# One small tile to the front, two padded: every SBUF tile of 1 KB or more starts at the same place modulo 256 bytes

## The chip, the cores and the metric

The kernel runs on one core of a Trainium2 chip. The metric is the device time of one execution in microseconds (us). The core has a matrix engine (TensorE, PE in the profile; its weight loads are listed apart, as PEld), a vector engine (VectorE, DVE), a scalar engine (ScalarE, ACT), GpSimd (POOL) and a queue engine (SyncE, SP). They work on SBUF, which has 128 partitions; a tile takes the same range of bytes in every partition, so a tile has one start address. Matmul results go to a separate memory, PSUM.

## What is computed

The reference is a one-layer encoder on a sequence of 1024 tokens with 1024 channels, all in float32. With depth 1 only the Hyena mixer is used, then a SwiGLU block, then a final norm:

```python
h = rmsnorm(x, norm_mix)
z = short_conv(h @ w_in + b_in, conv_w, conv_b)        # 1024 -> 3072, width 3
x0, x1, v = split(z, 3)
s = v * x1
g = hyena_filter(...)                                   # two-sided filter, L1-normalised
y = irfft(rfft(s, 2 * L) * rfft(g, 2 * L))[:L]          # long convolution
x = x + ((y + s * skip) * x0) @ w_out + b_out
x = x + (silu(u @ w_gate) * (u @ w_up)) @ w_down        # u = rmsnorm(x, norm_ffn), hidden 2816
return rmsnorm(x, norm_final)
```

## The kernel before

**Products.** Almost all of the work of TensorE is one kind of product. A float32 operand is split in a high part (a float32r copy, by ScalarE) and a low part (the difference, by VectorE or by an accumulating DMA on GpSimd's queue), and three products high·high, high·low and low·high are summed in PSUM. One such matmul takes a 128x128 block as stationary operand (the weight load) and streams a moving operand of 512 columns past it. The kernel has 4308 of these wide float32r matmuls, at six lines:

- lines 140, 356 and 683 (`gemm`, `piece`, `second_half`): z, the projection to 3072 channels, 1152 matmuls. The moving operand is the normed input, held in four tiles `uh0`, `uh1`, `ul0`, `ul1`; the stationary one is a block of `w_in` in a tile `whl`, which stands in the slot `whl0` or `whl1` (once in `cr`).
- line 895 (`out_mm`): po, the product with `w_out`, 384 matmuls. Here the `uh`/`ul` tiles are stationary and the `w_out` parts `wohl` are moving.
- line 1153 (`Unit.product`): the gate and up products. 22 units (`wg0` to `wg10`, `wu0` to `wu10`) of seven products `a` to `g`, of 12 matmuls each: 1848. The split weight is stationary and is put in turn in the five slots `fwd2`, `vz`, `s1`, `xz`, `sT` (`OPS`). The moving operand is `uh`/`ul`, or one of the sums T1 (slots `ab_g`, `gg0`), T2 (`cr`, `fwd01`), T3 (`whl1`, `hs`, `wt`).
- line 1397 (`mms`): bx, by and bz, the down products, 924 matmuls. The hidden values `hop` are stationary, `w_down` in `wop` is moving; both go through four pairs of slots in turn (`SETS`: `gg1`/`ab_d`, `hw`/`ss`, `inv`/`whl0`, and the pair `x0`,`ct_g` / `s0`,`ct_d`).

The other matmuls are narrower: transforms of 128 columns (lines 530, 531, 604, 643, 644), filter taps of 256 columns (513, 514) and transposes.

**Stages.** Up to about 430 us the kernel goes through eight channel blocks, one `period(b)` each: filter taps (ph), the filter's transform (pg), the turned signal (pst), its transform (pp), a butterfly on VectorE, the inverse transform (py) of the block before, and in between the z products of the next blocks, in stretches of 12, 6, 30 and 96 wide matmuls. Then the po products with the residual sum and the second norm (to about 557 us), the gate and up products (to about 955 us), and the down products with the final norm. The order on each engine is written out by hand (`manual_schedule`).

**Where tiles stand.** The pool `sb` gives each tag one slot (`bufs=2`: two), laid out in the order in which the tags are first asked for; a slot takes its size rounded up to 32 bytes. So one small tile in the row shifts all slots behind it. The start addresses that follow, modulo 256:

| slots | start modulo 256 before |
|---|---|
| `uh0`, `uh1`, `ul0`, `ul1`, `ident` | 128 |
| `fwd01`, `fwd2`, `ct_g`, `ct_d`, `ab_d`, `ab_g`, `x0`, `gg0`, `gg1`, `ss`, `cr`, `inv`, `wt`, `hs` | 96 |
| `junk`, `fw`, `dc`, `sT` | 128 |
| `s0`, `s1` | 192 |
| `xz`, `whl0`, `vz`, `whl1`, `fwh`, `fwl`, `hw` | 0 |

All offsets used inside these tiles by the wide matmuls are multiples of 512 bytes, so a matmul's two operands start modulo 256 where their slots start. In 784 of the 4308 wide matmuls the two starts are equal modulo 256 (432 of line 1153, 352 of line 1397), in the other 3524 they differ.

The small tiles that the change touches are `turn` (4 bytes, a factor for the filter's sine, used at line 709 and in `mlp_turns`), and the scratch of the norms, `rstd_of` (line 172 on, tags `rs1` and `rs2`) and `normed` (line 1038 on, tag `rs1`).

Of the kernel before, what the change touches and what calls it, by code (L numbers as in the profile page):

```python
# [102 lines left out]
def hyena_ffn_kernel(ctx: ExitStack, tc: tile.TileContext, a: dict, out: bass.AP):  # L103
# [18 lines left out]
    def small(name, *shape, tag=None, bufs=1, dt=F32):  # L122
        return sb.tile([P, *shape], dt, tag=tag or name, name=name, bufs=bufs)
# [38 lines left out]
    ones = small("ones", 1)  # L162
    V.memset(ones, 1.0)
    epst = small("epst", 1)
    V.memset(epst, EPS)
    warm = small("warm", 1)
    S.sqrt(warm, ones)

    def rstd_of(ss, n, nm):
        w = small(nm, 3 * n, tag=f"rs{n}", bufs=2)  # L170
        rt, r0, q = (w[:, i * n : (i + 1) * n] for i in range(3))
        S.activation(rt, ss, AF.Sqrt, bias=epst)
        V.reciprocal(r0, rt)
        V.scalar_tensor_tensor(q, ss, EPS, r0, ALU.add, ALU.mult)
        V.scalar_tensor_tensor(q, q, -0.5, r0, ALU.mult, ALU.mult)
        V.scalar_tensor_tensor(r0, q, 1.5, r0, ALU.add, ALU.mult)
        return r0
# [99 lines left out]
    rs = {}  # L277

    def rstd(j, n=1):
        r = rstd_of(sums[:, j : j + n], n, f"ra{j}")  # L280
        for q in range(n):
            rs[j + q] = r[:, q : q + 1]
# [41 lines left out]
            stop=True,  # L324
        )

    turn = small("turn", 1)

    def mlp_turns(li):
        ar = half(ark, li)  # L330
# [587 lines left out]
    b, f = NB - 1, F_[NB - 1]  # L918
# [117 lines left out]
        tops[nm] = (hi, lo)  # L1036

    def normed(j):
        w = small(f"rq{j}", 4, tag="rs1", bufs=2)
        sc, rt, r0, q = (w[:, i : i + 1] for i in range(4))  # L1040
        V.scalar_tensor_tensor(sc, sq2[j][:, 1:2], 1.0 / D, sq2[j][:, 0:1], ALU.mult, ALU.add)
        S.sqrt(rt, sc)
        V.reciprocal(r0, rt)
        V.scalar_tensor_tensor(q, sc, -0.5, r0, ALU.mult, ALU.mult)
        V.tensor_tensor(q, q, r0, ALU.mult)
        V.scalar_tensor_tensor(r0, q, 1.5, r0, ALU.add, ALU.mult)
        for h in range(2):
            d = x1[j][:, h * 512 : (h + 1) * 512]
            V.scalar_tensor_tensor(d, d, r0, gffn[:, h * 512 : (h + 1) * 512], ALU.mult, ALU.mult)
# [167 lines left out]
    with tc.manual_schedule(  # L1217
# [3 lines left out]
        for n, j in enumerate(seq):  # L1221
# [18 lines left out]
            if n < 7:  # L1240
                post_late()
                normed(j)
# [13 lines left out]
        ug.sums(V)  # L1256
        low_dma(pq[:, 0, 0], pq[:, 0, 1], ug.a12)
        normed(7)
        early_op(pq[:, 1], uu_.a12)
        ug.p1(pre[:, 0])  # L1260
# [263 lines left out]
```

## Time and profile before

| | |
|---|---|
| median of 3 runs (lowest, highest) | 1206.6 us (1204.96, 1207.47) |
| the profiled execution's own time | 1206.03 us |
| its span, first to last instruction | 1204.2 us |
| mean granted TensorE clock | 0.994 of full speed |
| PE busy | 1178.9 us, 98% of the span |
| DVE, ACT, POOL busy | 876.2, 516.1, 151.6 us |

The profile lists groups of instructions by source line and tile names (buffer numbers left out), with count, busy time and mean duration of one. Matmuls overlap in the pipeline and their ends are modelled, so the duration of one (near 390 ns for a wide one) is longer than the distance between the starts of two; the pace is read from start to start.

### The profile page before, as it was taken

To read this page: it belongs to the slowest core of one execution; us is meant where nothing else is said; L and a number is where in the kernel's file an instruction comes from. 1 tells how busy PE (TensorE), PEld (TensorE's weight loads), DVE (VectorE), ACT (ScalarE), POOL (GpSimd) and SP (SyncE) were. 2 spreads that over 40 slices of the span, in tenths; PEclk is the share of its full clock that TensorE was granted. 3 is DMA by queue.
4 is the path that set the end of the run, shared out by engine and by line. 5 is a ranking of instruction groups with operands and counts; after the bars stand their busy time and mean duration, and the time that the engine had idled before them with its cause. 6 is when DMAs were issued, how large, how long until landed. Compare 5 with 4: busy or idle time off the path is not lost.

```text
span 1204.2 us, 15168 instructions
## 1 busy us (share of the span) xinstructions
PE 1178.9 (98%) x5728; PEld 973.1 (81%) x5728; DVE 876.2 (73%) x1414; ACT 516.1 (43%) x818; POOL 151.6 (13%) x216
## 2 busy tenths in 40 slices
PE   8999999999999999998999999999999989999997
PEld 6788898888988887776888888888888868888885
DVE  6788989889898894588747666566656467955675
ACT  6564543545445472465233322332323233334444
POOL 0011211112011140043101110011001101111000
PEclk9999999999999999999999999999999999999999
DMA  7555667777575799443313332223323359832323
GB/s 218 158 114 130 144 162 161 166 152 164 125 154 108 199 244 262 132 114 70 131 44 123 100 128 88 88 97 122 105 71 108 111 180 350 311 117 92 96 79 140
DMA packets 100568, 170.32 MB, mean 141 GB/s; under 512 B 7052, under 2 KB 60684, under 8 KB 100367
## 3 DMA queue, kind: packets, MB, share of 16 engines
q0 software_dynamic: 24832, 78.39, 28.0%
q1 hardware_dynamic: 75661, 90.96, 22.8%
q8 instruction: 45, 0.74, 0.3%
q14 instruction: 28, 0.23, 0.1%
q10 hardware_dynamic: 2, 0.00, 0.0%
HBM read 101.96 MB, written 40.11 MB: 118 GB/s over the span
## 4 chain that ended last, share of the span: by engine, by line
PE 51%; DVE 3%; DMA 2%; ACT 1%; issue 1%; POOL 0%; SPq 0%; ACTq 0%; POOLq 0%
PE bx L1397 9%; PE by L1397 5%; PE bz L1397 3%; PE wg0dc L1153 1%; DMA hrp<-hd 1%; PE po L895 1%; PE wg1dc L1153 1%; PE wu8dc L1153 1%; PE wu5dc L1153 1%; PE wu3dc L1153 1%; PE wg6dc L1153 1%; PE wu7dc L1153 1%; PE wu2dc L1153 1%; PE wu9dc L1153 1%; PE wg5dc L1153 1%
## 5 line engine op out<-in xcount | busy, mean ns | idle before, releaser
L140 PE MATMUL z<-uh,whl 128*128 128x512 f32 x704 | 199.1, 398 | 0.2 <-DVE vz L386 0.2
L140 PEld LDWEIGHTS z<-uh,whl 128*128 128x128 f32 x704 | 130.4, 189 | 28.7 <-PE ph L514 0.4
L1397 PE MATMUL bx<-wop,hop 128*128 128x512 f32 x480 | 113.2, 394 | 1.4 <-ACT hop L129 1.1
L140 PE MATMUL z<-ul,whl 128*128 128x512 f32 x352 | 110.1, 394 | 0.0
L1397 PEld LDWEIGHTS bx<-wop,hop 128*128 128x128 f32 x480 | 89.9, 188 | 23.6 <-ACT hop L129 1.5
L130 DVE TENSOR_TENSOR hop<-hrp,hop 128x1024 fp32r<-128x1024 f32 (+1 forms) x40 | 45.1, 1129 | 52.1 <-ACT hop L129 52.0
L129 ACT CAST hop<-hrp 128x1024 fp32r<-128x1024 f32 (+1 forms) x40 | 38.9, 975 | 95.3 <-PE bx L1397 46.9
L895 PE MATMUL po<-wohl,uh 128*128 128x512 f32 x256 | 77.0, 403 | 2.0 <-DVE sig L659 1.8
L140 PEld LDWEIGHTS z<-ul,whl 128*128 128x128 f32 x352 | 66.3, 188 | 15.6
L1008 POOL DMA_DIRECT2D hd<-g x40 | 21.7, 545 | 332.8 <-DVE g L1313 193.7
L1397 PE MATMUL by<-wop,hop 128*128 128x512 f32 x264 | 61.5, 394 | 0.0
L895 PEld LDWEIGHTS po<-wohl,uh 128*128 128x128 f32 x256 | 48.1, 191 | 13.9 <-DVE sig L659 2.0
L1397 PEld LDWEIGHTS by<-wop,hop 128*128 128x128 f32 x264 | 49.6, 188 | 11.5
L190 ACT CAST whl<-wt 128x1024 fp32r<-128x1024 f32 x24 | 25.1, 1048 | 69.4 <-PE z L140 67.2
L129 ACT CAST wop<-wd 128x512 fp32r<-128x512 f32 x73 | 42.3, 617 | 18.7 <-PE by L1397 9.5
L150 POOL DMA_DIRECT2D whl<-wt x24 | 20.8, 872 | 229.2 <-ACT whl L149 218.8
L531 PE MATMUL pg<-hw,fwd 128*128 128x128 f32 x256 | 49.5, 275 | 0.0
L530 PE MATMUL pg<-hw,fwd 128*128 128x128 f32 x256 | 49.5, 275 | 0.0
L130 DVE TENSOR_TENSOR wop<-wd,wop 128x512 fp32r<-128x512 f32 x73 | 47.6, 685 | 2.0 <-ACT wop L129 2.0
L1008 POOL DMA_DIRECT2D hrp<-hd x42 | 22.4, 534 | 191.3 <-DVE hop L130 170.6
L895 PE MATMUL po<-wohl,ul 128*128 128x512 f32 x128 | 45.5, 400 | 0.0
L530 PEld LDWEIGHTS pg<-hw,fwd 128*128 128x128 f32 x256 | 39.5, 192 | 0.7
(1584 smaller groups left out, 2847.1 us busy)
## 6 DMA issues: line engine op xcount, KB each, us to landing
hrp<-hd POOLq DMA_DIRECT2D x35, 512.0 KB, 4.1
wt<-in_hy_w_in_dram SPq DMA_DIRECT2D x24, 512.0 KB, 4.9
whl<-wt POOLq DMA_DIRECT2D x24, 512.0 KB, 4.5
wgr<-in_ffn_w_gate_dram SPq DMA_DIRECT2D x22, 512.0 KB, 4.0
wur<-in_ffn_w_up_dram SPq DMA_DIRECT2D x22, 512.0 KB, 4.1
wd<-in_ffn_w_down_dram SPq DMA_DIRECT2D x44, 256.0 KB, 6.4
hd<-g POOLq DMA_DIRECT2D x40, 256.0 KB, 2.6
hd<-sx POOLq DMA_DIRECT2D x30, 256.0 KB, 2.7
```

The costliest lines, as they stand in the source:

```text
L129: S.copy(hi, src)
L130: (eng or V).tensor_tensor(lo, src, hi.bitcast(F32), ALU.subtract)
L140: T.matmul(pt[:, h * 512 : (h + 1) * 512], w[wi], u2[ui][h][:, k, :], start=first and ti == 0, stop=last and ti == len(TERMS) - 1,)
L150: G.dma_start(lo.bitcast(F32), src, accum_op=ALU.add)
L190: S.copy(whl[:, 0], w_raw[n])
L530: T.matmul(o, fwd[r][:, j, :], f.hw[:, j, 0, :], start=True, stop=False)
L531: T.matmul(o, fwd[2 * r][:, jj, :], f.hw[:, jj, 1, :], start=False, stop=True)
L895: T.matmul(o, u2[yi][th][:, k, m * P : (m + 1) * P], wos[h][k // 2][wi][:, k % 2, :], start=(k == 0 and ti == 0), stop=(k == NB - 1 and ti ...
L1008: G.dma_start(dst, src)
L1153: T.matmul(pt, t[:, wi, k, :], b(k)[ui], start=first and k == 0 and ti == 0, stop=k == 3 and ti == len(TERMS) - 1, skip_group_check=not first,
L1397: T.matmul(pt, ho[hi_][:, x, q * P : (q + 1) * P], wo_[wi][:, x, :], start=fresh and first and x == 0 and ti == 0, stop=last and x == n - ...
```

## The change

The tag `turn` is now asked for with the first small tiles, ahead of `fwd01`, instead of behind `hs`. That pushes `fwd01` to `hs` up by 32 bytes and leaves what comes behind where it was. The scratch tiles `rs1` and `rs2` (two buffers each) grow from at most 24 to 128 bytes, of which only the first few are used as before: `s0` and `s1` move up by 192 bytes, `xz` and all behind it by 384.

```diff
     epst = small("epst", 1)
+    turn = small("turn", 1)
     V.memset(epst, EPS)
...
     def rstd_of(ss, n, nm):
-        w = small(nm, 3 * n, tag=f"rs{n}", bufs=2)
+        w = small(nm, 32, tag=f"rs{n}", bufs=2)
...
-    turn = small("turn", 1)
...
     def normed(j):
-        w = small(f"rq{j}", 4, tag="rs1", bufs=2)
+        w = small(f"rq{j}", 32, tag="rs1", bufs=2)
```

Every slot of the table above then starts at 128 modulo 256. Modulo 512 they start at 128 too, but for `s0` and `s1`, which start at 384. Both operands of all 4308 wide matmuls start equal modulo 256; in 392 of them (those with `s0` or `s1`) they differ by 256 modulo 512. Each engine's list of instructions, with its shapes, waits and order, is the same as before; only addresses differ. The 1-column operands move too: `cp` from 224 to 0, the norms' scratch and the last small tiles by some bytes.

## The prediction

> **What bounds the kernel now.** First the page's head and busy shares:
>
> ```profile
> span 1204.2 us, 15168 instructions
> PE 1178.9 (98%) x5728; PEld 973.1 (81%) x5728; DVE 876.2 (73%) x1414; ACT 516.1 (43%) x818; POOL 151.6 (13%) x216
> PEclk9999999999999999999999999999999999999999
> ```
>
> TensorE works 98% of the span at the full granted clock. A change that moves only addresses shortens the kernel if it shortens matmuls, lengthens it if it lengthens them, and nothing else weighs as much. So the second view is the groups of matmuls by line:
>
> ```profile
> L140 PE MATMUL z<-uh,whl 128*128 128x512 f32 x704 | 199.1, 398 | 0.2 <-DVE vz L386 0.2
> L140 PE MATMUL z<-ul,whl 128*128 128x512 f32 x352 | 110.1, 394 | 0.0
> L530 PE MATMUL pg<-hw,fwd 128*128 128x128 f32 x256 | 49.5, 275 | 0.0
> L644 PE MATMUL py<-inv,vv 128*128 128x128 f32 x128 | 24.7, 275 | 0.0
> ```
>
> The z products, 1056 at this line, waited 0.2 us in all. The last two rows settle the narrow matmuls: pg pairs `hw` (0) with `fwd` (96), py pairs `inv` with `vv` (both 96), unequal against equal start, and both take 275 ns. Only the wide ones can be touched.
>
> The third view is the same group list for the gate and up stage, where each product is a row of its own and the five weight slots give every pairing of starts:
>
> ```profile
> L1153 PE MATMUL wg3ab<-uh,wg3b 128*128 128x512 f32 x8 | 2.7, 396 | 0.0
> L1153 PE MATMUL wu1ab<-uh,wu1b 128*128 128x512 f32 x8 | 2.7, 395 | 0.0
> L1153 PE MATMUL wg7ab<-uh,wg7a 128*128 128x512 f32 x8 | 2.7, 394 | 0.0
> L1153 PE MATMUL wu4ab<-T2h,wu4f 128*128 128x512 f32 x8 | 2.6, 390 | 0.0
> L1153 PE MATMUL wu3ab<-uh,wu3b 128*128 128x512 f32 x8 | 2.6, 390 | 0.0
> L1153 PE MATMUL wg2ab<-uh,wg2a 128*128 128x512 f32 x8 | 2.6, 390 | 0.0
> L1397 PE MATMUL bx<-wop12s,hop12x 128*128 128x512 f32 x8 | 3.2, 395 | 0.0
> L1397 PE MATMUL bx<-wop12ct_d,hop12x 128*128 128x512 f32 x8 | 3.1, 390 | 0.0
> ```
>
> Wg3b stood in `s1` (192), wu1b in `vz` (0), both against `uh` (128): 395 to 396 ns. Wg2a and wu3b stood in `sT` (128), equal to `uh`: 390. Wu4f in `fwd2` against T2 in `cr` and `fwd01`, 96 and 96: 390 too, so it is the equality and not the place. The last two rows are the cleanest: the same stationary blocks in `x0` (96) at the same time, with the moving part in `s0` (192) or in `ct_d` (96): 395 against 390. Wg7a, in `sT` like wg2a, shows 394; it is the exception that has to be explained. Single products by themselves, with minimum, median and maximum:
>
> ```profile
> L1153 PE MATMUL wg2ab<-uh,wg2a x8: 389/389/396, 613.2 to 615.7; 128*128 128x512 f32 x8
> L1153 PE MATMUL wg7ab<-uh,wg7a x8: 389/394/398, 808.2 to 811.2; 128*128 128x512 f32 x8
> L1153 PE MATMUL wu1ab<-uh,wu1b x8: 392/394/404, 615.9 to 618.5; 128*128 128x512 f32 x8
> ```
>
> Wg2a runs at a constant 389, with one exception; wu1b, unequal, wanders between 392 and 404 and never reaches 389. Wg7a reaches 389 but not at once: with equal starts the matmuls fall into a fast pace after some matmuls (I read none to ten of the twelve), and until then they wander like the others.
>
> A duration is modelled, so the chain of waits, which follows the matmuls through this stage from start to start, checks it, and the busy time of a stretch by windows gives the settled pace:
>
> ```profile
> 499.39 5.60 PE po L895 x24
> ...
> 604.96 5.58 PE wg1dc L1153 x24
> ...
> 613.34 2.73 PE wg2ab L1153 x12
> 616.07 2.80 PE wu1ab L1153 x12
> ...
> 1012.15 30.57 PE by L1397 x132
> ```
>
> ```profile
> 600.00:780.00 180.00, 180.00 (x777) 145.60 (x776) 112.41 (x164) 55.03 (x85) 15.97 (x30) 1.00 0.29 99
> 780.00:950.00 170.00, 170.00 (x734) 137.54 (x733) 108.29 (x156) 50.22 (x78) 17.33 (x33) 1.00 0.28 95
> 1090.37:1094.68 4.31, 4.31 (x20) 1.00 0.39 112
> 1083.82:1089.45 5.63, 5.63 (x26) 1.00 0.32 100
> ```
>
> From start to start wu1b took 2.80/12 = 233.3 ns, wg2a 2.73/12 = 227.5 with its exception. The third window lies in a down product with `gg1`/`ab_d` (96, 96): one of its 20 matmuls was under way at its beginning, so 19 started in 4.31 us, 226.8 ns each. The fourth, with `inv`/`whl0` (96, 0): 24 full ones in 5.63 us, 234.6 ns. I take 226.8 as the pace of a settled wide matmul with equal starts.
>
> **The change part by part.** The moved `turn` and the padding cost nothing by themselves: no instruction is added, none changes place. The sum has one gain and two deductions.
>
> The gain, by stage. For z a stretch of 96 shows the present pace:
>
> ```profile
> 128.58 1.10 PE L140 MATMUL z<-uh,whl 128*128 128x512 f32 x4
> 149.50 0.63 PE L140 MATMUL z<-uh,whl 128*128 128x512 f32 x2
> ```
>
> Between these two starts lie 90 matmuls in 20.92 us, 232.4 ns. So 1152 z matmuls gain 5.6 ns each, 6.5 us. For po the chain has 24 in 5.60 us, 233.3 ns: 384 by 6.5 is 2.5 us. In the gate and up stage 350 us hold 776 and 733 starts, 231.9 ns with the equal pairs in it: 1848 by 5.1 is 9.4 us. In the down stage 132 in 30.57 us are 231.6 ns: 924 by 4.8 is 4.4 us. Together 22.8 us, if every wide matmul ran settled.
>
> First deduction: settling. After a change to narrow matmuls, or a wait, the pace must be found again. One z period has stretches of 6, 12, 30 and 96 matmuls; with eight periods, the shorter stretches of po and the waits between the stages I count 57 stretches. At none to ten unsettled matmuls of 5.7 ns each that is 0 to 3.2 us. I take six, 2.0 us, since wg7a lies nearer to the long end than to none.
>
> Second deduction: places where TensorE does not set the end. The chain shows two; of po it holds the piece above and one more, and later it goes through DMAs:
>
> ```profile
> 532.59 5.61 PE po L895 x24
> ...
> 956.37 5.82 DMA hrp<-hd
> ...
> 985.55 5.40 DMA hrp<-hd
> ...
> 993.39 18.77 PE bx L1397 x80
> ```
>
> From about 492 to 557 us the norm's steps on VectorE and ScalarE alternate with po, and from 956 to 993 the reload of the hidden values is waited for. In these 102 us some 400 starts would fit at 232 ns, 2.3 us of the gain; on the chain in the first of them stand two pieces of 24, and after 967 us a few more, so not all of it is lost. I take 1.3 us lost, between 0.3 and 2.3.
>
> Cover. In the z stage VectorE is nearly full, and a faster TensorE leans on it. The tap product (line 520) must be done before pg:
>
> ```profile
> 102.90 0.17 DVE L521 MEMSET hw<- 1x128 f32 x1
> 103.92 0.38 PE L530 MATMUL pg<-hw,fwd 128*128 128x128 f32 x2
> DVE hw L520 <- PE ph L514: 6.3, 6, 1.1
> ```
>
> In the second period VectorE is 0.85 us early for pg; in the six later ones it waits 6.3/6 = 1.05 us for TensorE just before. Between pp and pg stand 138 wide matmuls, at 5.6 ns 0.77 us, less two settlings about 0.7. That fits in both; were the cover gone, the z gain would go with it (a rival below).
>
> VectorE's, ScalarE's and the DMAs' own operations read the moved tiles too. The rows nearest to a price: the high copies of wg2a (into 128) and of wu1b (into 0), and the same accumulating DMA into a slot at 0 and one at 96:
>
> ```profile
> L129 ACT CAST wg2a<-wgr x1: 620/620/620, 605.0 to 605.0; 128x512 fp32r<-128x512 f32 x1
> L129 ACT CAST wu1b<-wur x1: 620/620/620, 610.6 to 610.6; 128x512 fp32r<-128x512 f32 x1
> vz<-taps POOLq DMA_DIRECT2D x10, 512.0 KB, 5.0
> x<-taps POOLq DMA_DIRECT2D x9, 512.0 KB, 5.2
> ```
>
> The copies are equal, and the DMAs differ by 0.2 us at most, either way; their landings lie off the path in the z stage, where TensorE waits for none of them. I take nothing. The page "DMA: Bandwidth & Descriptors" of the Trainium skill, section "How a descriptor splits into AXI transactions", has a rule against this part: a transfer that doesn't start at a multiple of 256 bytes fetches from the boundary below, so slots moved from 0 to 128 (`whl0`, `vz`) would need 132 beats for 128, about 3%; an estimate by that rule is 0.15 us on a 5 us transfer, off the path, and no run here shows it.
>
> Sum: 22.8 - 2.0 - 1.3 = 19.5 us. Against the profiled execution's 1206.0 us that gives 1186.5 us; the median of the runs shown is 0.6 us higher, which is inside what a measurement can tell (0.2%, 2.4 us).
>
> **The rivals.** *No effect*: the pace of a wide matmul is not a matter of addresses, and the 390s are chance of the neighbours. Then nothing moves: 1206.0. Against it stand the two bx rows that differ in the moving slot alone. This is what the Trainium skill would say: "TensorE: Matmul & The Clock Gate", section "Step-by-step: what each phase is for", gives TensorE two independent read ports and says that loading the next weights takes nothing from the running matmul. By that rule the sum is 0; the rows at 389 and 394 don't agree with it.
>
> *VectorE becomes the bound of the z stage*: the 0.85 and 1.05 us are partly hand-over time, and the period keeps its length. Of the z gain (6.5 less 1.1 for settling) nothing comes: 1206.0 - 19.5 + 5.4 = 1191.9. For it speaks that VectorE runs through most of a period; against it the wait of 1.05 us, longer than the gain.
>
> *The step is 512, not 256*: `s0` and `s1` then stay slow. 392 matmuls by 6.2 ns are 2.4 us, and each of the some 30 products in `s1` unsettles the next, 6 by 5.7 ns, 1.0 us: 1189.9. Nothing in the profile decides; before, every equal pair was equal modulo 512 too.
>
> *Slower*: the pace belongs to certain pairs of slots, and bringing all starts to one place gives everything the worst wandering that the trace shows, 234.6 ns (`inv`/`whl0`), instead of the 232.1 to which the four paces above average. 4308 by 2.5 is 10.8 us: 1216.8. It would decide at the first long stretch of z: above 232.4 ns per start the kernel is slower. For it speaks wg7a, equal and yet at 394; against it that four pairs of different slots all reach 389 or 390.
>
> That the change doesn't do what it says is excluded by the layout.
>
> **How the numbers follow.** The forecast 0.76, the 512 step 0.07, VectorE's bound 0.07, no effect 0.06, slower 0.04. Faster by over 0.2%: 0.76 + 0.07 + 0.07 = 0.90; within 0.2% 0.06; slower 0.04. The low end of the range is the full 22.8 us without a deduction, 1183; the high end is settling at ten (1.2 more), the chain's loss at 2.3 (1.0 more) and either the 512 step or VectorE's bound, about 1193. No effect and slower are left out, 0.1 in all.
>
> **What would show it.** Right: z, po, gate/up and down rows with mean durations near 390 instead of 394 to 398; 96 z starts in 21.9 us instead of 22.4; 132 by starts in 29.9 us instead of 30.57; pg, py and the copies unchanged at 275 and 620 ns. VectorE's bound would show as waits of pg for `hw`; the 512 step as products in `s1` that stay at 395. Wrong: z rows that stay at 394 and more, or rise.

## The result and the profile after

The changed kernel takes 1187.0 us (median of 4 runs, 1184.94 to 1188.58) against 1206.9 us of the kernel before beside it (4 runs, 1204.96 to 1207.47). The ratio is 0.9837, 95% interval 0.9817 to 0.9857. The profiled execution of the changed kernel took 1186.09 us. Its page's head and busy shares:

```profile
span 1184.2 us, 15168 instructions
PE 1157.2 (98%) x5728; PEld 971.6 (82%) x5728; DVE 875.1 (74%) x1414; ACT 516.6 (44%) x818; POOL 151.3 (13%) x216
PEclk9999999999999999999999999999999999999999
```

The number of instructions is the same, and VectorE's and ScalarE's busy times moved by about 1 us. TensorE's busy time fell by 21.7 us, the span by 20.0. The groups of matmuls by line, after:

```profile
L140 PE MATMUL z<-uh,whl 128*128 128x512 f32 x704 | 195.4, 392 | 0.3 <-DVE vz L386 0.3
L140 PE MATMUL z<-ul,whl 128*128 128x512 f32 x352 | 108.7, 390 | 0.0
L1397 PE MATMUL by<-wop,hop 128*128 128x512 f32 x264 | 60.2, 389 | 0.0
L1153 PE MATMUL wg3ab<-uh,wg3b 128*128 128x512 f32 x8 | 2.6, 389 | 0.0
L1153 PE MATMUL wu1ab<-uh,wu1b 128*128 128x512 f32 x8 | 2.6, 389 | 0.0
L1397 PE MATMUL bx<-wop12s,hop12x 128*128 128x512 f32 x8 | 3.1, 389 | 0.0
L530 PE MATMUL pg<-hw,fwd 128*128 128x128 f32 x256 | 49.4, 275 | 0.0
L514 PE MATMUL ph<-fwl,hs 128*128 128x256 f32 x64 | 15.7, 283 | 0.0
```

Every wide group came down to 389 to 392 ns, the narrow pg stayed at 275, and one group that the prediction did not price got slower: the ph matmuls of 256 columns went from 280 to 283 ns. Their row before:

```profile
L514 PE MATMUL ph<-fwl,hs 128*128 128x256 f32 x64 | 15.4, 280 | 0.0
```

The single products, with minimum, median and maximum:

```profile
L1153 PE MATMUL wg7ab<-uh,wg7a x8: 389/389/389, 798.2 to 801.2; 128*128 128x512 f32 x8
L1153 PE MATMUL wg3ab<-uh,wg3b x8: 389/389/389, 665.0 to 667.5; 128*128 128x512 f32 x8
```

Wg7a no longer wanders: now the products before it have equal starts too, so it can begin at the settled pace. From start to start, the timeline of the z stretch of 96 and the chain in the down stage:

```profile
128.50 1.08 PE L140 MATMUL z<-uh,whl 128*128 128x512 f32 x4
148.92 0.61 PE L140 MATMUL z<-uh,whl 128*128 128x512 f32 x2
```

```profile
494.98 6.97 PE po L895 x24
...
1055.95 29.92 PE by L1397 x132
```

Ninety z matmuls take 20.42 us, 226.9 ns each (232.4 before), and 132 down matmuls 29.92 us, 226.7 each (231.6 before). One line went the other way: 24 po matmuls on the chain at 494.98 us took 6.97 us where the piece at 499.39 us took 5.60 before. The waits of TensorE and VectorE, after, show what stands ahead of it and what became of the cover; first the row of the transposes (`tp`) before:

```profile
PE tp L1054 <- DVE x L1049: 1.7, 2, 1.5
```

```profile
PE tp L1054 <- DVE x L1049: 3.3, 1, 3.3
...
PE po L895 <- DVE sig L659: 1.8, 1, 1.8
```

```profile
DVE hw L520 <- PE ph L514: 2.6, 6, 0.4
```

VectorE still waits for TensorE ahead of the tap product, 0.43 us each time instead of 1.05, so TensorE still sets the z stage. The wait of the transposes for the normed tokens (`x`, line 1049) grew from 1.5 to 3.3 us, and behind it the clock fell. The profile's rows by windows show that, after:

```profile
494.60:498.00 3.40, 3.40 (x11) 2.72 (x9) 2.14 (x8) 2.74 (x5) 0.00 (x0) 0.50 0.21 77
498.00:502.00 4.00, 4.00 (x20) 3.24 (x20) 0.22 (x2) 0.00 (x0) 0.00 (x0) 1.00 0.00 0
```

The last three columns are the granted clock, the DMA share and GB/s: 0.50 for 3.4 us, then 1.00. The kernel before has such stretches too, in other places:

```profile
469.70:472.70 3.00, 3.00 (x8) 2.31 (x7) 1.29 (x2) 2.88 (x4) 0.00 (x0) 0.50 0.76 155
968.00:971.00 3.00, 3.00 (x8) 2.32 (x7) 2.85 (x4) 2.19 (x5) 0.53 (x1) 0.50 0.10 19
```

In them a wide matmul takes 426 ns from start to start; seven of them cost 1.4 us. After the first 55 us, the first profile of before had three (7 each, near 470, 559 and 968 us), that of after one (6, near 495).

**Where the time went.** With the same 5728 matmuls in the same order, each distance between two starts can be set against its counterpart. Sorted into wide matmuls that follow one another at full clock, those at half clock, and the rest (waits, changes of width), the two first profiles differ by, in us:

| stretch | all | wide, full clock | half clock | waits and the rest |
|---|---|---|---|---|
| up to the z loop (54 us) | +0.85 | -0.26 | 0 | +1.10 |
| z | -4.86 | -4.93 | 0 | +0.07 |
| po and second norm | +0.62 | -1.89 | -0.20 | +2.72 |
| gate and up, to the first down products | -12.91 | -10.32 | -2.71 | +0.12 |
| down | -3.74 | -4.20 | 0 | +0.47 |
| sum | -20.04 | -21.60 | -2.91 | +4.48 |

So the gain is the pace of the wide matmuls. Of the two other columns, -2.9 and +4.5 us, the prediction had neither at that size; together they take 1.6 us back.

### The profile page after: what moved, and what is told of

It reads as the page before. It is cut to its first block, busy times and chain, and to the rows that moved or that the text cites. A ratio compares the mean times of both kernels' runs of the same rounds, so it can differ in the third digit from the quotient of the medians.

```text
span 1184.2 us, 15168 instructions
## 1 busy us (share of the span) xinstructions
PE 1157.2 (98%) x5728; PEld 971.6 (82%) x5728; DVE 875.1 (74%) x1414; ACT 516.6 (44%) x818; POOL 151.3 (13%) x216
## 3 DMA queue, kind: packets, MB, share of 16 engines
q1 hardware_dynamic: 75661, 90.96, 23.4%
## 4 chain that ended last, share of the span: by engine, by line
PE 46%; DVE 6%; DMA 4%; issue 2%; ACT 1%; SPq 0%; POOL 0%; DVEq 0%; POOLq 0%; ACTq 0%
PE bx L1397 7%; PE bz L1397 3%; PE by L1397 3%; DMA wd<-in_ffn_w_down_dram 2%; PE po L895 1%; PE wu9dc L1153 1%; PE wu7dc L1153 1%; PE wu5dc L1153 1%; PE wg9dc L1153 1%; PE wu8dc L1153 1%; PE wg8dc L1153 1%; PE wg7dc L1153 1%; PE wu6dc L1153 1%; PE wg6dc L1153 1%; PE wg5dc L1153 1%
## 5 line engine op out<-in xcount | busy, mean ns | idle before, releaser
L140 PE MATMUL z<-uh,whl 128*128 128x512 f32 x704 | 195.4, 392 | 0.3 <-DVE vz L386 0.3
L1008 POOL DMA_DIRECT2D hd<-g x40 | 21.6, 543 | 323.2 <-DVE g L1313 187.8
L1397 PEld LDWEIGHTS by<-wop,hop 128*128 128x128 f32 x264 | 49.5, 188 | 10.3
L191 ACT CAST whl<-wt 128x1024 fp32r<-128x1024 f32 x24 | 25.2, 1049 | 67.9 <-PE z L140 64.7
L150 POOL DMA_DIRECT2D whl<-wt x24 | 20.8, 871 | 221.1 <-ACT whl L149 120.9
```

Source lines behind the costliest of these rows:

```text
L140: T.matmul(pt[:, h * 512 : (h + 1) * 512], w[wi], u2[ui][h][:, k, :], start=first and ti == 0, stop=last and ti == len(TERMS) - 1,)
L150: G.dma_start(lo.bitcast(F32), src, accum_op=ALU.add)
L191: S.copy(whl[:, 0], w_raw[n])
L1008: G.dma_start(dst, src)
L1397: T.matmul(pt, ho[hi_][:, x, q * P : (q + 1) * P], wo_[wi][:, x, :], start=fresh and first and x == 0 and ti == 0, stop=last and x == n - ...
```

## Experiments

The theory: a wide float32r matmul runs at 226.7 ns from start to start when its two operands start at the same place modulo 256 bytes, and wanders around 229 to 235 ns otherwise. The rivals: the step is 512, or certain slots are slow, or a certain place (128) is fast, or the padding and the moved tile do something of their own.

**The pace by itself.** A probe runs nothing but matmuls, 48 a section, back to back, with a chosen distance between the operands' starts; it leaves out the whole computation of the reference.

```diff
+for d in (0, 4, 8, 16, 32, ..., 240, 252, 256, 384, 512, 768):
+    section(f"d{d}w", [(0, d, 512)], 48)     # moving start, stationary start (bytes), columns
+section("both36x", [(36, 36, 512)], 48)
+section("ownx", [(0, 0, 512), (128, 128, 512)], 48)
+section("nextx", [(0, 128, 512), (128, 0, 512)], 48)
```

> A probe that leaves out the whole computation of the reference: it only issues stretches of 48 wide float32r matmuls (128x128 stationary, 512 moving columns, fixed addresses, nothing to wait for), each stretch with one difference d between the start of the stationary and of the moving operand. Theory (a common start modulo 256 lets the matmul settle): d = 0, 256, 512, 768 settle at 226.7 ns from start to start, mean duration near 389; every other d, 128 included, stays at 231 to 235 ns on average, near 394 to 398. Both at 128 and both at 36 bytes are like both at 0. Open, and read off here: whether a difference of 4 to 16 bytes already counts (theory as worded: yes), whether some d is faster than 0 (not expected), and whether the stationary block that matters is the matmul's own or the next one, which is loaded while it runs: if the next, the stretch 'own' (own pair equal, next unequal) is slow and 'next' is fast; if the own, the other way round. Rival (certain slots are fast, not the equality): no order by d at all. Rival (the two reads never meet, as two independent ports would have it): every stretch the same, whatever d.

Single sections of this probe, with minimum, median and maximum, and first and last start:

```profile
L36 PE MATMUL d0w<-mv,w x48: 389/389/397, 27.0 to 37.7; 128*128 128x512 f32 x48
L36 PE MATMUL d32w<-mv,w x48: 390/395/397, 71.4 to 82.3; 128*128 128x512 f32 x48
L36 PE MATMUL d96w<-mv,w x48: 392/397/400, 116.1 to 127.1; 128*128 128x512 f32 x48
L36 PE MATMUL d128w<-mv,w x48: 392/396/398, 138.5 to 149.5; 128*128 128x512 f32 x48
L36 PE MATMUL d192w<-mv,w x48: 388/392/394, 183.1 to 193.9; 128*128 128x512 f32 x48
L36 PE MATMUL d256w<-mv,w x48: 389/389/396, 238.3 to 248.9; 128*128 128x512 f32 x48
L36 PE MATMUL both36x<-mv,w x48: 397/400/402, 326.2 to 337.4; 128*128 128x512 f32 x48
```

Forty-seven distances between the first and the last start: 10.7 us give 227 ns, 11.0 give 234, 11.2 give 238. From the single records of the settled half, distances of 0, 256, 512 and 768 give 226.7 ns; 32 to 64, 112, 128 and 160 give 233.3, 96 gives 234.4, 192 gives 228.9. Not all came out as expected: 8 and 176 (230.7 and 230.0 ns) also lie below the 231 to 235 that had been given for every unequal distance, and 240 and 252, where the stationary block starts 16 and 4 bytes ahead modulo 256, settle at 226.7 ns. So it is, these two apart, the distance modulo 256, in a kernel without any other engine at work: the 512 step, the slots and contention with other engines' reads are ruled out as the cause. Two starts that are equal but stand 36 bytes behind the tiles' start are slowest of all, 237.8 ns: equal starts alone are not enough. Alternating sections, in which either the own or the next stationary block is equal, came out between (228.3 and 230.0 ns), so which of the two loads matters stays open.

**Half the change each.** Each half of the change alone:

```diff
 # moved tile alone: the scratch tiles as before
-        w = small(nm, 32, tag=f"rs{n}", bufs=2)
+        w = small(nm, 3 * n, tag=f"rs{n}", bufs=2)
-        w = small(f"rq{j}", 32, tag="rs1", bufs=2)
+        w = small(f"rq{j}", 4, tag="rs1", bufs=2)
```

> Only the moved tile, without the padding: the slots from fwd01 to hs at 128, s0 and s1 at 192, xz and all behind at 0. Equal pairs go from 784 to 1448 of 4308: po in three of four parts, 760 instead of 432 in the gate and up stage, z almost none. Theory: po gains 288 by 5.5 ns, 1.6 us; the 328 of the gate and up stage lie in products of 12 between unequal ones and settle late, 3 ns each, 1.0 us; about 1204.3 us (1203.0 to 1205.5), 2.6 below before. Rival (place 128 for the moving operand or the stationary one by itself is what pays): the down stage, where the most slots move to 128, and T1, T2 would gain too, about 1198.

```diff
 # padding alone: turn where it stood before
-    turn = small("turn", 1)          # ahead of fwd01
+    turn = small("turn", 1)          # behind hs
```

> Only the padding, without the moved tile: fwd01 to hs stay at 96, s0, s1, xz and all behind go to 128. Equal pairs go from 784 to 2672: 1104 of 1152 z, 96 of 384 po, 1120 of 1848 in the gate and up stage, down unchanged. Theory: z gains about 5.3 us, po 0.5, the gate and up stage 688 by 3 to 5.7 ns, 2.1 to 3.9; about 1198.3 us (1196.5 to 1200), z rows at 390, down rows still at 394. The gains of the two halves alone (2.6 and 8.6) then fall short of the 20 of both, since equality is a matter of pairs. Rival (each tile gains by itself): the two halves add up to 20.

The moved tile alone makes 1448 of the 4308 matmuls equal and took 1204.1 us (10 runs; ratio 0.9978, 0.9966 to 0.9990). The padding alone makes 2672 equal and took 1197.3 us (0.9919, 0.9900 to 0.9939). Beside them ran the kernel before, 1206.4 us. First the moved tile's z rows, then the padding's z and by rows:

```profile
L140 PE MATMUL z<-uh,whl 128*128 128x512 f32 x704 | 198.8, 397 | 0.2 <-DVE vz L386 0.2
L140 PE MATMUL z<-ul,whl 128*128 128x512 f32 x352 | 110.1, 394 | 0.0
```

```profile
L140 PE MATMUL z<-uh,whl 128*128 128x512 f32 x704 | 195.7, 393 | 0.3 <-DVE vz L386 0.3
L140 PE MATMUL z<-ul,whl 128*128 128x512 f32 x352 | 108.8, 390 | 0.0
L1397 PE MATMUL by<-wop,hop 128*128 128x512 f32 x264 | 61.4, 394 | 0.0
```

The padding brings `whl` to the place of `uh` and so speeds z; the pairs of the down stage stay apart and stay at 394. Together the halves are worth 2.3 + 9.1 = 11.4 us, the whole 19.9: a product gains only when both of its tiles are at one place, which no theory of single slots or of the padding itself gives.

**All starts at another place.** A small tile of 128 bytes ahead of `uh0` brings all the big slots to 0 modulo 256.

```diff
+    first = small("first", 32)
+    V.memset(first, 0.0)
     u2 = [
```

> The changed kernel with 128 bytes more ahead of all tiles: every slot of 1 KB or more starts at 0 modulo 256 instead of 128, all pairs stay equal. Theory: as after, 1187.0 us within the runs' spread. Rival (128 is a good place): back towards 1207. By the page DMA: Bandwidth & Descriptors of the Trainium skill (how a descriptor splits into transactions) transfers would become about 3% shorter; they are off the path, so no change of the time, and whl<-wt would land in 4.4 instead of 4.5 us.

It took 1188.0 us (0.9837, 0.9817 to 0.9857), as the changed kernel. The place doesn't matter, 0 or 128. The prediction cited a rule of the Trainium skill, "DMA: Bandwidth & Descriptors", section "How a descriptor splits into AXI transactions"; an estimate by that rule has transfers that start at 128 take some 3% longer than those that start at 0. The transfers of `whl` in this run (slots at 0), then in the changed kernel (128):

```profile
whl<-wt POOLq DMA_DIRECT2D x24, 512.0 KB, 4.5
```

```profile
whl<-wt POOLq DMA_DIRECT2D x24, 512.0 KB, 4.6
```

The profile's tenths of a microsecond hide the size. To the nanosecond, the median of the 24 transfers is 4.45 us in this run and 4.61 to 4.65 in the three profiles of the changed kernel, and for `vz<-taps` it is 4.91 and 5.15 to 5.18. The kernel before, where `whl` mostly stood at 0 but the source `wt` at 96, lies between (4.55 to 4.59). So these transfers were 3 to 5% shorter with both ends at 0, which agrees with the rule in its direction and about in its size; the reload `hrp<-hd` shows no such difference (4.1 us here, 3.9 to 4.0 in the changed kernel). There is one profile at 0 only, and none of this is on the path.

**The edges, other types, and settling.** The second probe, again without the reference's computation:

```diff
+section(f"lead{d}w", [(256, 256 - d, 512)], 48)   # stationary 4 to 64 bytes ahead
+section(f"place{r}x", [(r, r, 512)], 48)          # both at the same odd place
+section(f"half{d}x", [(0, d, 256)], 48)           # 256 columns
+section(f"bf{d}x", ...); section(f"plain{d}x", ...)  # bfloat16; plain float32
```

> A second probe, again without the reference's computation. (1) lead4 to lead64: the stationary block starts 4 to 64 bytes ahead of the moving one. The first probe settled at 16 and 4 bytes ahead and not at 32 ahead or 4 behind; so up to 16 should settle at 226.7 ns, and the edge lies between 16 and 32. (2) place4 to place96: both at the same odd place. The first probe had 237.8 ns with both 36 bytes on; if that is the break of 16-byte lines, 4, 8, 12 and 20 are slow and 16, 32, 48, 64, 96 run at 226.7; if every place but a multiple of 32 is slow, 16 and 48 are slow too. (3) un/eq and vn/fq: stretches of 25, 26 and 27 unequal matmuls, each followed by 24 equal ones: the equal ones should settle within ten. (4) half: 256 columns wide. The first probe had 120.0 ns for equal and 118.7 for 128 apart; so the rule should not hold at this width, and the spread over d should stay within 3 ns. (5) bf: bfloat16, 512 wide: theory says nothing; if the common start matters there too, d = 0 differs from the others. (6) plain: float32 operands, where a matmul takes several passes: no difference expected, as for the narrow transforms.

```profile
L43 PE MATMUL lead4w<-mv,w x48: 389/389/396, 27.7 to 38.4; 128*128 128x512 f32 x48
L43 PE MATMUL lead8w<-mv,w x48: 393/396/401, 38.6 to 49.6; 128*128 128x512 f32 x48
L43 PE MATMUL place16x<-mv,w x48: 393/393/394, 205.5 to 216.3; 128*128 128x512 f32 x48
L43 PE MATMUL place32x<-mv,w x48: 389/389/400, 227.8 to 238.5; 128*128 128x512 f32 x48
L43 PE MATMUL place64x<-mv,w x48: 387/389/397, 249.8 to 260.5; 128*128 128x512 f32 x48
L43 PE MATMUL half0x<-mv,w x48: 278/283/283, 340.8 to 346.4; 128*128 128x256 f32 x48
L43 PE MATMUL half96x<-mv,w x48: 277/280/282, 357.9 to 363.4; 128*128 128x256 f32 x48
L43 PE MATMUL bf0x<-mb,wb x48: 379/379/390, 386.2 to 396.4; 128*128 128x512 bf16 x48
L43 PE MATMUL bf128x<-mb,wb x48: 379/379/379, 417.3 to 427.5; 128*128 128x512 bf16 x48
```

The places count from the start of the probe's tiles, which is 128 modulo 256. Equal starts settle at 226.7 ns 32, 64 and 96 bytes behind it, not at 4, 8, 12, 16, 20 or 48 (228.9 to 237.8). A stationary block 4 bytes ahead settles too; 8 or 12 ahead does not, and 16 ahead settled in the first probe and stayed at 228.3 in this one. The two sections stood at other addresses and followed other sections; which of these decides was not tested. For 256 columns equal starts give 120.0 ns and 96 apart 117.4; that is the ph rows' 283 and 280 (from start to start 119.5 and 117.4 ns in the kernel). But 160 apart gives 120.0 as well, so equality by itself does not order the paces there. At 384 and 448 columns, in the first probe, equal starts are ahead of 128 apart again: 173.3 against 175.8 and 202.5 against 204.3 ns. Bfloat16 runs at 215.8 ns at all five distances tried, and plain float32 at 429.2 ns for each of a matmul's two records, at 0 and at 128. After an unequal stretch, an equal one wandered for 1 to 9 distances before the constant 226, 227, 227.

**Two placements more.** Thirty-two bytes between the `uh`/`ul` tiles and everything else leave the T sums' products and the down products equal (1716) and part all the others by 32 bytes; and eight gaps leave no pair equal at all.

```diff
+    gap = small("gap", 8)            # 32 bytes, behind uh and ul
+    V.memset(gap, 0.0)
     ident = small("ident", P)
```

> The changed kernel with 32 bytes put between the uh/ul tiles and all the rest: everything else still has a common start, but every product with uh or ul (z, po and 1056 of the gate and up stage, 2592 matmuls) has its two starts 32 bytes apart. Theory: z gives back 6.3 us, po 2.1, gate and up 6.8 and 1.3 more for the products between them that have to settle again, down nothing: 16.5 in all, about 1203.5 us (1201 to 1206), with the down rows still at 389 and z at 394 to 396. Rival (a shift of 32 bytes is small against 256 and still counts as the same place): 1187.

```diff
+    gaps = {"fwd01": 1, "fwd2": 1, "ct_g": 1, "x0": 2, "junk": 1, "s0": 1, "xz": 5, "whl1": 5}
     def slot(tag, name, shape=(1024,), dt=F32):
+        n = gaps.pop(tag, 0)
+        if n:
+            sb.tile([P, 8 * n], F32, tag=f"gap_{tag}", name=f"gap_{tag}")
```

> The changed kernel with gaps of 32 to 160 bytes between groups of tiles, so that none of the 4308 wide matmuls has equal starts (before had 784, after 4308). Theory: all at about 233 ns, 6.3 above the settled pace; 4180 steady distances give 26 us of excess where the changed kernel has 1.6, and of such a difference 93% showed in the time (20.0 of 21.6): about 1210 us (1208 to 1213), slower than before by the share that the 784 equal pairs had been worth. Rival (before already had nothing to lose): 1206.9.

With the 32 bytes it took 1200.9 us (0.9941, 0.9926 to 0.9956), just below the range expected of it (1201 to 1206). The pace came as forecast: its wide starts at full clock lost 16.0 us against the first profile of the changed kernel, where z, po, gate and up were to give back 16.5. But half clock and waits gave 3.1 us of it back, which the forecast had left out. Within one kernel, products side by side show both paces:

```profile
L1155 PE MATMUL wg2ab<-uh,wg2a x8: 395/396/397, 615.2 to 617.8; 128*128 128x512 f32 x8
...
L1155 PE MATMUL wg2ab<-T2h,wg2f x8: 389/390/398, 626.3 to 634.4; 128*128 128x512 f32 x8
```

Thirty-two bytes are as bad as 128. With no pair equal the time is 1208.3 us (10 runs, 1204.9 to 1212.1; ratio 1.0009, 0.9993 to 1.0025). That is in the range of 1208 to 1213, but it can't be told from before either, so the time leaves the rival (1206.9) standing. The starts decide: the excess over 226.7 ns a wide start, summed, is 25.1 us here and 23.2 to 23.4 in the three profiles of the kernel before. So the 784 equal pairs were worth some 2 us only, of the 4.9 that 6.3 ns each would make. They stood in stretches of at most 24 among unequal ones and ran, in the first profile, at 230.1 ns in gate and up and 228.4 in the down stage, so that much of their gain was spent on settling.

**The clock.** The first two profiles differ by 2.9 us in half-clock matmuls. To see whether that belongs to the change, both kernels were profiled twice more, with no edit.

> The changed kernel once more, unaltered. Its first profile held one stretch of half clock after 60 us (6 matmuls at 426 ns near 495 us), that of the kernel before three (7 each near 470, 559 and 968 us), 2.9 us between them. Theory: where the clock halves is a matter of each execution, not of the change; then this profile may show another number of stretches (0 to 3, about 1.5 us each), at the same few waits, and the span follows it: 1184.2 plus 1.5 us, less what waits absorb, for each stretch more. Its wide matmuls still run at 226.7 ns, z rows at 390 to 392. Rival: the change itself removes two stretches; then again one, near 495, and a span within 0.5 us of 1184.2.

> The kernel before once more, unaltered. Theory (the clock halves by the execution): some number of stretches from 0 to 3, possibly other than the three of its first profile, and a span of 1204.2 less about 1.5 us for each stretch fewer, 1199.5 at the least. Rival (three stretches belong to the old layout): three again, near 470, 559 and 968 us, and 1204 within 0.5 us plus the start's scatter of 1 us. z rows at 394 to 398 in both.

> As the first repeat of the changed kernel, a third profile of it. Theory: the three profiles of the changed kernel don't all show the same stretches. Rival: all three show one stretch near 495 us alone.

> As the first repeat of the kernel before, a third profile of it. Theory: the three profiles of the kernel before don't all show the same stretches. Rival: all three show the same three.

The changed kernel took 1185.95 and 1185.39 us, the kernel before 1206.65 and 1205.71, with 1205.46 in the run beside them. Of the kernel before, the second profile had half-clock stretches near 470, 559 and 993 us, the third near 501 and 561 only; the changed kernel had one near 495 us, of 5 matmuls, both times. So for the kernel before the place and number differ from one execution to the next. For the changed kernel they did not in three, where another outcome had been expected. And a stretch fewer did not shorten the span by 1.5 us: the third profile of the kernel before has two and spans 1203.9 us, the first has three and spans 1204.2. The waits show why. In the second and in the third profile of the kernel before:

```profile
PE tp L1054 <- DVE x L1049: 1.6, 1, 1.6
```

```profile
PE tp L1054 <- DVE x L1049: 3.0, 1, 3.0
```

In the eleven profiles of full kernels it goes one of two ways. Either the clock halves near 470 us, TensorE comes late to the transposes and waits 1.5 to 1.6 us there, with no drop behind it (two of before, and the kernel without equal pairs); or it does not, TensorE waits 2.9 to 3.3 us, and the clock halves then, for one to eight matmuls (the other eight).

What makes the clock halve can be narrowed down from the traces, which list the granted clock by times. After 55 us every stretch of half clock lasts 3.41 us, and every stretch of full clock between two of them a whole multiple of that (85.3 us is 25 times, 406.2 us 119 times). So the clock seems to be set for one window of 3.41 us at a time, on a grid that does not follow the program's waits. Along this grid, the eleven profiles have 3626 windows between 55 us and the last 15 us of the span. TensorE was busy for less than 46% of 20 of them, and each of these is followed by a window of half clock. Of the windows above 48% none is. Seven lie at 47.4%, of which three are followed by half clock and four (near 460 us, in the changed kernel and in the one with the padding alone) are not. In the kernel before, whose profiles all have a wait of 1.8 us near 468 us, that wait halves the clock where it falls into one window and not where it is cut in two by the grid. The first profile of the kernel before, and then the third, by such windows (the first number behind the length is the busy time of TensorE):

```profile
466.13:469.54 3.41, 1.61 (x8) 1.20 (x8) 2.51 (x2) 1.33 (x3) 0.86 (x1) 1.00 1.04 391
469.54:472.95 3.41, 3.41 (x10) 2.62 (x9) 1.29 (x2) 3.04 (x4) 0.05 (x1) 0.50 0.73 151
```

```profile
465.58:468.99 3.41, 2.17 (x20) 1.98 (x18) 0.78 (x1) 2.10 (x2) 0.05 (x1) 1.00 0.99 354
468.99:472.41 3.42, 2.86 (x12) 2.36 (x13) 2.70 (x4) 1.62 (x3) 0.81 (x1) 1.00 1.07 314
```

This is read from traces, whose matmul ends are modelled; no run moved a wait on purpose. Over the nine pairs of a before and an after profile, the pace is worth 21.4 to 21.7 us, everything else (half clock, waits and the start) takes back between 0.4 and 2.0, and the start scatters within 1.5 us in both kernels (the z loop began at 54.1, 55.1 and 55.3 us before, at 54.9, 54.9 and 53.8 after). The Trainium skill, "TensorE: Matmul & The Clock Gate", section "What's actually happening", has a window of about 3.4 us that runs free of the program and decides between half and full clock; the stretches of 3.41 us and their grid agree with it. The Trainium skill, "TensorE: Matmul & The Clock Gate", section "Why this matters for your kernels", asks for no gaps over about 3 us; here gaps of 1.8 to 2.6 us halved the clock too, where they left TensorE busy for less than about half of one window.

## Why the prediction was right, and where its sum was not

- *The rule itself* held. With equal starts modulo 256 the wide matmuls settle at 226.7 ns (226.8 was taken). The probe, the halves, and the layouts at 0, 32 bytes apart and with no pair equal all follow it, but for the exceptions that the probes found (4 bytes ahead, places off a multiple of 32).
- *The gain and the settling*, 22.8 - 2.0 = 20.8 us, measured 21.6. The settling that is left is 1.6 us, the excess of all wide starts at full clock over 226.67 ns; that is five matmuls a stretch where six were taken. By stages the wide starts gained 5.2 us in z (with those ahead of the loop), 1.9 in po, 10.3 in gate and up, 4.2 in down, settling included. Only gate and up, taken at 9.4, was sized too low: the count of a window holds the matmuls that were under way at its beginning, and by single starts 1684 of them gained 9.35 us, 5.55 ns each, not 5.1.
- *The second deduction*, 1.3 us, failed as an argument, though not in its net size. Its 102 us hold 440 starts at 232 ns, not some 400. Of its two places, the second norm (492 to 557 us) lost more than taken: waits and the rest grew by 2.7 us there in the first pair of profiles. The reload of the hidden values (956 to 993 us) lost nothing; from the last gate and up products into the first down products the changed kernel took 2.7 us less, half of it by a half-clock stretch that this execution did not have. The granted clock stood in no term of the sum: the page's row of nines, from which the prediction read full clock, has slices of 30 us, in which 3.4 us at half leave a nine. That 1.3 us lies near the 1.6 us by which all but the pace fell short (+4.5 and -2.9 us) is luck, and the nine pairs of profiles have between 0.4 and 2.0.
- *Cover.* VectorE stayed ahead, with little to spare: in the second period the clearing ends 0.12 us before pg starts (below), where it was 0.85, and the waits of line 520 went from 1.05 to 0.43 us. That z gained its pace in spite of it rules out VectorE's bound. The timeline of the changed kernel, VectorE's row and TensorE's:

```profile
103.67 0.17 DVE L521 MEMSET hw<- 1x128 f32 x1
...
103.96 0.38 PE L530 MATMUL pg<-hw,fwd 128*128 128x128 f32 x2
```

- *The rivals.* No effect is refuted by the result. The rule behind it, of two read ports that don't disturb each other (the Trainium skill, "TensorE: Matmul & The Clock Gate", section "Step-by-step: what each phase is for"), does not agree with the probe for float32r: 226.7 against 233.3 ns with nothing changed but the place of the weights. By which path the place acts is open. The step of 512 is refuted by the distances 256 and 768 of the probe, and by wg3b in `s1`, now 389. The slower case, slots that belong together, is refuted by the layout at 0 and by wg7a, which stayed in `sT` and now runs at 389.
- *The narrow matmuls* were called untouched on the strength of the ones of 128 columns. Those of 256 columns (ph, 128 matmuls) were not looked at and took 0.5 us more busy time, on the wrong side.

Open: why the distance matters. That the two reads of SBUF get in each other's way would fit, but no run here shows it.

## What to carry to other kernels

Where TensorE is the bound and works in single-pass float32r with 512 columns, lay both operands of every matmul at the same place modulo 256 bytes, a multiple of 32 (0, 128, 160, 192 and 224 were tried); it was worth 2.8% of a wide matmul's time (233.3 to 226.7 ns) and 1.6% of this kernel's, and costs a few small tiles of padding. Make all pairs equal at once, since short equal products among unequal ones lose much of their gain on settling, and don't expect it of bfloat16, plain float32 or 256 columns. When a kernel with waits gets faster, compare the granted clock around those waits before putting the rest of the difference down to the change.

## What had not been expected of the hardware

- Equal starts are no help off a multiple of 32 bytes; both operands 4 or 36 bytes off are worse than any unequal pair tried (237.8 ns against 234.4).
- At 256 columns equal starts are among the slow cases: 120.0 ns, as at 160 bytes apart, against 117.4 to 118.8 at the other six distances.
- Float32r at its best took 226.7 ns for 512 columns, bfloat16 215.8 at every distance tried.
- The clock halves for one window of 3.41 us at a time, and it did so behind every such window in which TensorE was busy for less than 46%. Whether a wait of 1.8 us costs a half-clock stretch (1.4 us for seven matmuls) so depends, among other things, on how the wait falls on the windows, and that changed between executions of the same kernel.
